# Expert weights in loads of 2 MB, and the conditional part of a mixture-of-experts layer behind pair 10

## The chip, the core and the metric

The kernel runs on one core of one Trainium2 chip. The metric is device time in microseconds for one execution of the whole layer; the median of three runs is given. Engines are TensorE (PE for matmuls, PEld for its weight loads), VectorE (DVE), ScalarE (ACT), GpSimd (POOL) and SyncE (SP); SP issues nearly all transfers from memory.

## What is computed

One layer of a hybrid decoder on 256 tokens of width 1024. A mixer (stick-breaking attention beside an mLSTM, gated and projected) comes first, then a mixture of 32 experts, top 4 of them for each token, then a final RMSNorm. The expert part carries most of the bytes:

```python
def clamped_swiglu_expert(xb, w1, b1, w2, b2):
    a = xb @ w1 + b1
    x_glu, x_lin = jnp.split(a, 2, axis=-1)
    x_glu = jnp.minimum(x_glu, SWIGLU_LIMIT)
    x_lin = jnp.clip(x_lin, -SWIGLU_LIMIT, SWIGLU_LIMIT)
    return ((x_lin + 1.0) * (x_glu * jax.nn.sigmoid(SWIGLU_ALPHA * x_glu))) @ w2 + b2
...
top_logit, top_idx = lax.top_k(logits, TOP_K)
top_w = jax.nn.softmax(top_logit, axis=-1)
...
y = jnp.zeros((n_tok, d), h.dtype).at[row_tok].add((rows * row_w[:, None]).astype(h.dtype))
```

Each expert has `w1` of 1024 x 2048 and `w2` of 1024 x 1024 in float32, 12.6 MB together; all 32 experts are read, 403 MB.

## The kernel before

**Mixer.** Up to about 375 us the kernel computes the mixer. Its weights come through the function `load` into weight buffers of 8 KB per partition (1 MB, called a slot here): 16 in the first stage, then 41 chunks of projection weights and 16 blocks of modulation weights, 73 in all. `next_slot` hands out slots in a fixed rotation over four pools (`ring` 8, `ring2` 4, `ring3` 5, `ring4` 1, and one named `mglo` from `mgp`), 19 at the end. A load into a slot waits until the last reader of what stood there is done. SP issues loads in a fixed order, so one that waits holds up all that stand behind it.

**Experts.** Experts are taken two at a time, 16 pairs. A pair has 24 weight tiles of 1 MB: 8 of `w1` for half 0 of the hidden width (hf 0), 8 for half 1 (hf 1), 8 of `w2` (kt 0 to 7 each). `pair(p)` puts the biases into PSUM (`biases`), runs `first_product` for hf 0 with the scatter of the pair before (`scatter`, behind kt 1 to 4), then hf 1, then gathers the tokens of the next pair (`gather`), then runs `second_product`. One tile feeds four matmuls of 128x512, each recorded as two. Each of the two experts has room for 64 tokens.

**Prefetch for pair 0.** While the router is computed, 16 of the loads of pair 0 are in flight or landed; the two tiles of kt 7 of `w1` go as 256 KB pieces into small buffers of the pool `spl`, and kt 5 of `w2` goes as two pieces into `spare` and `more_rows`.

**Conditional part.** Experts with more than 64 tokens would be served by `more` in two nested loops under `tc.If(rounds > 0)`. Here `rounds` is 0 and nothing of it runs, but each engine loads the number `nit` and branches over the body. Five slots (`ws`) are taken for it. It stands behind pair 14. Ahead of it the scatter of pair 14 runs alone and the eight hf 0 loads of pair 15 are issued. Instructions are reordered by the compiler within the code ahead of the conditional and within the code behind it, not across it.

**Last pair.** Pair 15 is written out by hand: hf 0, the map for its scatter, hf 1, and then `steps`, in which the second product comes in three column groups (512, 256, 256) with the output work of each group (`out_of`) between them, from `w2_last` in pieces of 1 MB and 512 KB. The RMSNorm and the store end the kernel.

Of the kernel before, what the change touches and what calls it, by code (L numbers as in the profile page):

```python
# [13 lines left out]
F32 = mybir.dt.float32  # L14
# [10 lines left out]
D = 1024  # L25
# [38 lines left out]
def body(tc, a, out):  # L64
# [17 lines left out]

    const, c_const = pool("const")
    ring, c_ring = pool("ring", bufs=RING)
    slots, SLOT_NAME = [ring] * RING, {}

    def next_slot(shape):

        p = slots.pop(0)
        slots.append(p)  # L90
        return p.tile(shape, F32, name=SLOT_NAME.get(p, "w"))

    def load(src, shape):
        w = next_slot(shape)
# [585 lines left out]
    moe, c_moe = pool("moe", reuse_waits="tile")  # L680
    xgp, c_xgp = pool("xgp", reuse_waits="tile")
    ring3, c_ring3 = pool("ring3", bufs=RING3, reuse_waits="tile")
    ring4, c_ring4 = pool("ring4", side="right", reuse_waits="tile")
    slots[4:4] = [ring3] * RING3 + [ring4]
    wk, c_wk = pool("wk", reuse_waits="tile")
    table("natural_log_exp_and_others")
    A2 = moe.tile([128, 8], F32, name="A2")
# [201 lines left out]
        act(S, pt[:, 0:T], AF.Copy)  # L889
        SS[p] = S  # L890

    def of_w1(p, hf, kt):

        return load(w1[p, hf, kt], [128, 2, 2, 512])

    def of_w2(p, kt):

        return load(w2[p, kt], [128, 2, D])


    W1 = {(hf, kt): of_w1(0, hf, kt) for kt in range(7) for hf in range(2)}
# [1 line left out]
    for hf in range(2):  # L903
        W1[hf, 7] = [[spl.tile([128, 512], F32, name=("whi", "wlo")[hf]) for b in range(2)] for e in range(2)]
        for e in range(2):
            for b in range(2):
                nc.sync.dma_start(W1[hf, 7][e][b], w1[0, hf, 7, :, e, b])
    for kt in range(2, 5):
        W2[kt] = of_w2(0, kt)
    spare = xgp.tile([128, 1, D], F32, name="xh")  # L910
    nc.sync.dma_start(spare, w2[0, 5, :, 0:1])
    more_rows = next_slot([128, 1, D])
    nc.sync.dma_start(more_rows, w2[0, 5, :, 1:2])

    def biases(p):
        sel = wk.tile([128, 2, CAP], BF16, name="sel", bufs=2)
# [6 lines left out]

    def first_product(p, a1, hf, kt):

        w = W1.pop((hf, kt)) if p in (0, NE // 2 - 1) and (hf, kt) in W1 else of_w1(p, hf, kt)
        for b in range(2):
            for e in range(2):
                pe(a1[2 * b + hf][64 * e:64 * e + 64], XG[p][:, kt, 64 * e:64 * e + 64],
                   w[e][b] if isinstance(w, list) else w[:, e, b], start=False, stop=kt == KT - 1, skip_group_check=True)  # L930

    def second_product(p, a2, aT, kt):
        if p == 0 and kt == 5:
            w = [spare[:, 0], more_rows[:, 0]]
        else:
            w = W2[kt] if p == 0 and kt in W2 else of_w2(p, kt)
# [9 lines left out]
    def pair(p):  # L946
        a1 = biases(p)
        aT = halves([128, 4, 128]) if p else None
        if p == 0:
            for kt in range(KT):  # L950
                gather((kt,), G0, XG[0])
                for hf in range(2):
                    first_product(p, a1, hf, kt)
            scatter_map(p)
            aT = halves([128, 4, 128])
            ms = [hidden(a1, hf) for hf in range(2)]
            G, _ = slots_of(p + 1)
# [27 lines left out]
    def add_b2(b2):  # L985
# [8 lines left out]
    for p in range(NE // 2 - 1):  # L994
        pair(p)
        if p == 1:
            b2 = xgp.tile([128, D], F32, name="xh")[0:32]
            nc.sync.dma_start(b2, a["b2"])
        if p == 3:
            add_b2(b2)  # L1000
# [21 lines left out]
    def more(r, q, e, ws):  # L1022
# [21 lines left out]
        for kt in range(KT):  # L1044
            w = ws[kt % 4]
            for hf in range(2):
                nc.gpsimd.dma_start(w.rearrange("p (b h n) -> p b h n", b=2, h=2)[:, :, hf],
                                    w1[ds(q, 1), hf, kt, :, e].rearrange("q p b n -> p (q b) n"))
            for n in range(4):
                mm(a1[n], xg[kt // 4][:, kt % 4, :], w[:, 512 * n:512 * n + 512], start=False, stop=kt == KT - 1)  # L1050
        aT = activations(a1)
        a2 = [ps1.tile([128, 512], F32, name=f"s{n}") for n in range(2)]
        for kt in range(KT):
            w = ws[kt % 4]
            nc.gpsimd.dma_start(w[:, 0:D], w2[ds(q, 1), kt, :, e].rearrange("q p n -> p (q n)"))
# [5 lines left out]
    ws = [next_slot([128, 2 * D]) for _ in range(5)]  # L1061
    with tc.If(rounds > 0):
        with tc.For_i(0, rounds, 1) as r:
            with tc.For_i(0, NE // 2, 1) as q:
                for e in range(2):
                    more(r, q, e, ws)
# [12 lines left out]
    m = hidden(a1, 1)  # L1079
# [78 lines left out]
    close(c_ring4, c_mgp, c_ps2, c_ps1, c_wk, c_ring3, c_xgp, c_moe, c_ring2, c_mb, c_spl, c_m, c_ring, c_const)  # L1158


RING, RING2, RING3 = 8, 4, 5

LAST = ((0, 512, 2), (512, 256, 4), (768, 256, 2))


def layout(i):
# [28 lines left out]
    o["w1"] = np.ascontiguousarray(n["expert_w1"][0].reshape(16, 2, KT, 128, 2, 2, 512).transpose(0, 5, 2, 3, 1, 4, 6))  # L1195
    o["b1"] = n["expert_b1"][0]
    o["w2"] = np.ascontiguousarray(n["expert_w2"][0].reshape(16, 2, KT, 128, D).transpose(0, 2, 3, 1, 4))
# [22 lines left out]
```

## Time and profile before

| | us |
|---|---|
| median of 3 runs (1326.29 to 1328.52) | 1328.28 |
| the profiled execution, its own time | 1330.19 |
| its span from first to last instruction | 1328.5 |
| PE busy in the span | 1228.4 (92%) |
| DVE / ACT / POOL busy | 468.0 / 329.9 / 30.0 |
| read from memory | 481.21 MB, 363 GB/s over the span |

The profiled execution lies 1.9 us above the median; 1.7 us of its time lie outside the span. A busy PE is one with a matmul in flight, not one at its peak. The DMA share is the mean busy share of the core's 16 DMA engines. A wait for several semaphores is put down to the one that came last. A slice of the page is a fortieth of the span, 33.2 us.

### The profile page before, as it was taken

What the parts mean: (1) busy time and instruction counts of PE and PEld (TensorE: products, weight loads), DVE (VectorE), ACT (ScalarE), POOL (GpSimd) and SP (SyncE); (2) the same over time, 40 slices, a digit from 0 to 9 for tenths busy, and PEclk for the clock granted to TensorE, in tenths of its full rate; (3) what the DMA queues carried; (4) which work ended last, traced back from release to release, by engine and by line L of the source; (5) the groups of instructions that cost most, each with busy time, mean ns of one, the idle gap of its engine ahead of it and who ended that gap; (6) DMA issues with size and microseconds to landing.
All of it is one profiled execution on the core that took longest, in us unless ns stands there. A gap on an engine that the chain in (4) does not pass through costs nothing. (4 is left out here: it accounts for less than half of the span.)

```text
span 1328.5 us, 16889 instructions
## 1 busy us (share of the span) xinstructions
PE 1228.4 (92%) x6859; PEld 668.3 (50%) x6874; DVE 468.0 (35%) x923; ACT 329.9 (25%) x616; POOL 30.0 (2%) x63
## 2 busy tenths in 40 slices
PE   5979999999999999999999999988989898898787
PEld 3878999999963333433334433332333333332323
DVE  5979888776532112122121220212121120201203
ACT  4457767655522010110101101010110101010102
POOL 2000000000000000000000000000000000000002
PEclk8989999999999999999999999999999999999989
DMA  9586476486878999999999999999999999999993
GB/s 342 205 301 254 159 275 235 172 343 245 330 278 361 407 418 420 420 420 420 420 421 420 420 422 419 420 420 420 421 420 421 420 421 420 420 420 420 419 419 151
DMA packets 70337, 483.46 MB, mean 364 GB/s; under 512 B 8134, under 2 KB 9558, under 8 KB 13676
## 3 DMA queue, kind: packets, MB, share of 16 engines
q1 hardware_dynamic: 69084, 480.54, 89.3%
q0 software_dynamic: 624, 1.23, 0.3%
q8 instruction: 57, 0.93, 0.3%
q10 hardware_dynamic: 544, 0.52, 0.1%
q14 instruction: 28, 0.23, 0.0%
HBM read 481.21 MB, written 1.05 MB: 363 GB/s over the span
## 5 line engine op out<-in xcount | busy, mean ns | idle before, releaser
L808 PE MATMUL s<-w,xg 128*64 128x512 f32 x1928 | 450.2, 602 | 31.3 <-DMA w<-in_w 28.1
L808 PEld LDWEIGHTS s<-w,xg 128*64 128x64 f32 x1928 | 125.2, 137 | 296.9 <-issue 207.2
L808 PE MATMUL t<-w,whi 128*64 128x512 f32 x908 | 204.2, 596 | 13.4 <-ACT whi L859 9.6
L825 DVE SCALAR_TENSOR_TENSOR xT<-pm,modT,xT 128x256 f32<-128x256 f32 x128 | 56.0, 479 | 391.1 <-PE pm L808 391.1
L808 PEld LDWEIGHTS t<-w,whi 128*64 128x64 f32 x908 | 61.7, 137 | 133.9 <-issue 103.7
L843 ACT ACTIVATE wlo<-wlo 128x512 f32<-128x512 f32 x32 | 20.2, 630 | 425.3 <-DVE wlo L841 425.3
L222 DVE TENSOR_TENSOR wlo<-w,whi 128x512 fp32r<-128x512 f32 x164 | 110.0, 686 | 44.3 <-ACT whi L220 43.6
L220 ACT ACTIVATE whi<-w 128x512 fp32r<-128x512 f32 x162 | 100.8, 629 | 80.7 <-PE pj L257 61.9
L841 DVE TENSOR_SCALAR wlo<-s 128x512 f32<-128x512 f32 x32 | 22.1, 691 | 249.0 <-PE s L808 227.5
L258 PE MATMUL pj<-hhi,wlo 128*128 128x256 f32 x368 | 104.9, 285 | 0.9 <-DVE wlo L222 0.8
L256 PE MATMUL pj<-hhi,whi 128*128 128x256 f32 x368 | 105.0, 285 | 0.2 <-DVE kp L486 0.2
L257 PE MATMUL pj<-hlo,whi 128*128 128x256 f32 x368 | 104.5, 284 | 0.0
L258 PEld LDWEIGHTS pj<-hhi,wlo 128*128 128x128 f32 x368 | 70.4, 191 | 1.6 <-DVE wlo L222 1.4
L256 PEld LDWEIGHTS pj<-hhi,whi 128*128 128x128 f32 x368 | 70.4, 191 | 0.8 <-DVE kp L486 0.4
L257 PEld LDWEIGHTS pj<-hlo,whi 128*128 128x128 f32 x368 | 70.5, 192 | 0.3 <-issue 0.2
L808 PEld LDWEIGHTS pm<-G,mghi 128*128 128x128 f32 x512 | 59.0, 192 | 17.6 <-issue 17.0
L808 PE MATMUL pm<-S,whi 128*128 128x256 f32 x240 | 67.3, 404 | 0.2 <-DVE xT L825 0.2
L808 PEld LDWEIGHTS pm<-S,whi 128*128 128x128 f32 x240 | 40.8, 189 | 50.0 <-issue 37.1
L808 PE MATMUL pm<-G,mghi 128*128 128x128 f32 x512 | 63.3, 279 | 0.2 <-ACT xg L836 0.2
L169 DVE CUSTOM_DVE_ANT_0 w<-w,silr,col 128x1024 f32<-128x1024 f32 x48 | 60.4, 1278 | 1.1 <-DMA w<-in_ada 0.9
L859 ACT ACTIVATE whi<-pm 128x512 f32<-128x512 f32 x32 | 19.1, 598 | 166.8 <-PE pm L811 166.8
L836 ACT ACTIVATE xg<-pm,modT 128x128 f32<-128x128 f32 x128 | 37.1, 368 | 63.5 <-PE pm L808 63.5
(371 smaller groups left out, 1335.1 us busy)
## 6 DMA issues: line engine op xcount, KB each, us to landing
w<-in_w SPq DMA_DIRECT2D x354, 1024.0 KB, 19.9
w<-in_w_in SPq DMA_DIRECT2D x29, 1024.0 KB, 6.5
w<-in_ada SPq DMA_DIRECT2D x22, 1024.0 KB, 5.6
mglo<-in_w SPq DMA_DIRECT2D x19, 1024.0 KB, 19.9
w<-in_w_first SPq DMA_DIRECT2D x7, 896.0 KB, 12.9
w<-in_w_last SPq DMA_DIRECT2D x5, 1024.0 KB, 19.6
w<-in_w_a SPq DMA_DIRECT2D x4, 1024.0 KB, 5.3
w<-in_w_b SPq DMA_DIRECT2D x4, 1024.0 KB, 12.5
```

Source lines behind the costliest of these rows:

```text
L169: nc.vector.tensor_tensor_reduce(out=w[:, j + n, :], in0=w[:, j + n, :], in1=SILU[-1], scale=1.0, scalar=col[:, C_AB + i:C_AB + i + 1], op ...
L220: act(hi, x, AF.Copy)
L222: nc.vector.tensor_tensor(lo, x, f32(hi), OP.subtract)
L256: mm(ps[:, n, :], whi[:, j, s], mhi[:, kt, :], start=kt + n == 0, stop=False, skip_group_check=True)
L257: mm(ps[:, n, :], whi[:, j, s], mlo[:, kt, :], start=False, stop=False, skip_group_check=True)
L258: mm(ps[:, n, :], wlo[:, j, s], mhi[:, kt, :], start=False, stop=last, skip_group_check=True)
L808: return tc.keep_in_program_order(mm(*args, **kw))
L825: stt(xT[:, kt, :], p[:, j, :], mod_of(G2, kt), xT[:, kt, :], OP.mult, OP.add)
L836: act(xg[kt] if isinstance(xg, list) else xg[:, kt, :], p[:, width * j:width * j + width], AF.Identity, bias=mod_of(SH2, kt))
L841: ts(g, glu, LIMIT, None, op0=OP.min)
L843: act(s, g, AF.Sigmoid, scale=ALPHA)
L859: act(aT[hf], pt.rearrange("p (k m) -> p k m", k=4), AF.Copy)
```

## The change

Weight buffers become 16 KB per partition: `ring` 4, `ring2` 2, `ring3` 3, nine in all; `ring4` is gone, and `mglo` serves once, for kt 4 of `w2` of pair 0. `next_slot` now hands out halves of such a buffer (a wide buffer here), two calls for one; `next_wide` hands out a whole one and drops a half that is left over. `w1` and `w2` are laid out in memory so that two kt stand side by side, 16 KB in a row for each partition. For pairs 1 to 15 `first_product` loads two kt of `w1` in one transfer of 2 MB, and for pairs 1 to 14 `second_product` does so with `w2`. The mixer's loads, those of pair 0 and those of `w2_last` stay at 1 MB or less, into halves.

The conditional part stands behind pair 10. The scatter of pair 10 runs alone ahead of it, and pair 11 has none in its first product. The hand-written prefetch of eight loads for pair 15 is gone; the scatter of pair 14 runs inside hf 0 of pair 15, as in the other pairs, and the map for the scatter of pair 15 moves from behind hf 0 to behind kt 1 of hf 1.

```diff
-    slots, SLOT_NAME = [ring] * RING, {}
+    slots, spare_half = [ring] * RING, []
...
+    def next_wide():
+        spare_half.clear()
         p = slots.pop(0)
         slots.append(p)
-        return p.tile(shape, F32, name=SLOT_NAME.get(p, "w"))
+        return p.tile([128, 4 * D], F32, name="w")
+
+    def next_slot(shape):
+        if not spare_half:
+            w = next_wide()
+            spare_half.append(w[:, 2 * D:])
+            return shaped(w, shape)
+        return shaped(spare_half.pop(), shape)
...
-    slots[4:4] = [ring2] * RING2
+    slots[2:2] = [ring2] * RING2
...
-    ring4, c_ring4 = pool("ring4", side="right", reuse_waits="tile")
-    slots[4:4] = [ring3] * RING3 + [ring4]
+    slots[2:2] = [ring3] * RING3
...
-    SLOT_NAME[mgp] = "mglo"
-    slots.append(mgp)
...
+    def wide_w1(p, hf, k2):
+        w = next_wide()
+        nc.sync.dma_start(w, w1[p, hf, k2].rearrange("p j e b n -> p (j e b n)"))
+        return [shaped(w[:, 2 * D * j:], [128, 2, 2, 512]) for j in range(2)]
+
+    def wide_w2(p, k2):
+        w = next_wide()
+        nc.sync.dma_start(w, w2[p, k2].rearrange("p j e n -> p (j e n)"))
+        return [shaped(w[:, 2 * D * j:], [128, 2, D]) for j in range(2)]
...
-    for kt in range(2, 5):
+    for kt in range(2, 4):
         W2[kt] = of_w2(0, kt)
+    W2[4] = of_w2(0, 4, mgp.tile([128, 2, D], F32, name="mglo"))
...
-        w = W1.pop((hf, kt)) if p in (0, NE // 2 - 1) and (hf, kt) in W1 else of_w1(p, hf, kt)
+        if (hf, kt) not in W1:
+            W1[hf, kt], W1[hf, kt + 1] = wide_w1(p, hf, kt // 2)
+        w = W1.pop((hf, kt))
...
-                if 1 <= kt <= 4:
+                if p - 1 in ROWS and 1 <= kt <= 4:
                     scatter(p - 1, (kt - 1,))
...
-    p = NE // 2 - 1
-    scatter(p - 1)
-    for kt in range(KT):
-        W1[0, kt] = of_w1(p, 0, kt)
...
+    for p in range(NE // 2 - 1):
+        pair(p)
...
+        if p == REST_AT:
+            scatter(p)
+            del ROWS[p]
+            rest_of_slots()
+
+    p = NE // 2 - 1
     a1 = biases(p)
     aT = halves([128, 4, 128])
     for kt in range(KT):
         first_product(p, a1, 0, kt)
-    scatter_map(p)
+        if 1 <= kt <= 4:
+            scatter(p - 1, (kt - 1,))
     m = hidden(a1, 0)
     for kt in range(KT):
         first_product(p, a1, 1, kt)
+        if kt == 1:
+            scatter_map(p)
...
-RING, RING2, RING3 = 8, 4, 5
+RING, RING2, RING3 = 4, 2, 3
+REST_AT = 10
```

`rest_of_slots` holds what stood under the conditional before: five calls of `next_slot` for `ws`, the test and the two loops.

## Rows read from the trace of the kernel before

**Rows 1.** Page, part 2: busy tenths of 40 equal slices of the span
```profile
PE   5979999999999999999999999988989898898787
DMA  9586476486878999999999999999999999999993
GB/s 342 205 301 254 159 275 235 172 343 245 330 278 361 407 418 420 420 420 420 420 421 420 420 422 419 420 420 420 421 420 421 420 421 420 420 420 420 419 419 151
```

**Rows 2.** Windows: stretch, us, busy of each engine, PEclk, DMA share, GB/s
```profile
600.00:1200.00 600.00, 561.34 (x2605) 209.23 (x2614) 110.48 (x233) 64.32 (x152) 2.94 (x10) 1.00 1.01 420
```

**Rows 3.** Waits of the whole run: us in total, times, longest us
```profile
PEld s L808 <- DMA w<-in_w: 83.8, 85, 1.6
...
SPq L95 <- DMA w<-in_w: 600.4, 288, 3.5
```

**Rows 4.** Timeline of PE: start us, us, instructions, idle before them
```profile
442.28 0.81 PE L808 MATMUL s<-b1s,sel 128*128 128x512 bf16 x3 [0.16 <-issue]
...
496.12 0.81 PE L808 MATMUL s<-b1s,sel 128*128 128x512 bf16 x3 [0.16 <-issue]
...
1228.43 1.94 PE L808 MATMUL s<-w,xg 128*64 128x512 f32 x8 [0.55 <-DMA w<-in_w]
```

**Rows 5.** Chain that ended last, in order of time: start us, us, what
```profile
1265.56 17.66 PE s L808 x68
```

**Rows 6.** Timeline around the conditional part, 1248 to 1268 us
```profile
1248.40 17.80 SPq L95 DMA_DIRECT2D w<-in_w  x8
...
1250.25 1.99 PE L808 MATMUL pm<-S,whi 128*128 128x256 f32 x8
...
1259.96 0.98 DVE L884 TENSOR_SCALAR rw<-cst,rank,gate 128x64 f32<-128x64 f32 x4 [4.65 <-PEq L1062]
1265.56 1.87 PE L808 MATMUL s<-b1s,sel 128*128 128x512 bf16 x4 [11.15 <-issue]
```

**Rows 7.** Windows: one stretch of 10 us behind the branch
```profile
1260.00:1270.00 10.00, 4.44 (x12) 1.31 (x14) 0.95 (x4) 0.00 (x0) 0.00 (x0) 0.50 1.02 420
```

**Rows 8.** Windows: the last microseconds of the loads
```profile
1306.00:1308.00 2.00, 2.00 (x20) 1.12 (x16) 0.00 (x0) 0.60 (x1) 0.00 (x0) 1.00 0.33 133
1308.00:1309.00 1.00, 1.00 (x8) 0.69 (x5) 0.00 (x0) 0.00 (x0) 0.00 (x0) 1.00 0.06 25
```

**Rows 9.** Timeline of PE in the last pair's second product
```profile
1302.92 5.38 PE L1105 MATMUL t<-w,whi 128*64 128x512 f32 x32 [0.69 <-ACT whi L859]
...
1310.15 3.67 PE L1105 MATMUL t<-w,whi 128*64 128x256 f32 x32
...
1314.82 1.95 PE L1105 MATMUL t<-w,whi 128*64 128x256 f32 x16
```

**Rows 10.** DMA queues, 600 to 1200 us: packets, MB, share; loads: KB, us to landing
```profile
q1 hardware_dynamic: 34557, 251.66, 101.0%
q8 instruction: 21, 0.34, 0.2%
...
w<-in_w SPq DMA_DIRECT2D x226, 1024.0 KB, 19.9
```

**Rows 11.** DMA queues, 1323 to 1328 us, where the output is stored
```profile
q10 hardware_dynamic: 544, 0.52, 32.0%
q1 hardware_dynamic: 544, 0.52, 31.5%
```

**Rows 12.** Timeline of SP, 414 to 430 us
```profile
414.53 14.45 SPq L95 DMA_DIRECT2D w<-in_w  x3
```

**Rows 13.** Windows: one microsecond in pair 0
```profile
427.00:428.00 1.00, 1.00 (x6) 0.29 (x4) 0.27 (x2) 0.92 (x4) 0.00 (x0) 1.00 0.00 0
```

**Rows 14.** The tile nit: duration ns min/median/max, first and last start us
```profile
L1015 DVE CAST nit<-cnt x1: 143/143/143, 386.2 to 386.2; 1x1 int32<-1x1 f32 x1
...
L1016 SPq TENSOR_LOAD <-nit x1: 486/486/486, 1248.8 to 1248.8; - x1
...
L1016 PEldq TENSOR_LOAD <-nit x1: 494/494/494, 1253.2 to 1253.2; - x1
```

More of the change, by code (lines that the diff above doesn't have):

```diff
@@ L84, in body, with shaped @@
     ring, c_ring = pool("ring", bufs=RING)
-    slots, SLOT_NAME = [ring] * RING, {}
-    def next_slot(shape):
+    slots, spare_half = [ring] * RING, []
+    def shaped(x, shape):
+        n = int(np.prod(shape[1:]))
+        names = "abc"[:len(shape) - 1]
+        x = x[:, 0:n]
+        if len(names) == 1:
+            return x
+        return x.rearrange(f"p ({' '.join(names)}) -> p {' '.join(names)}", **dict(zip(names[1:], shape[2:])))
+    def next_wide():
+        spare_half.clear()
         p = slots.pop(0)
         slots.append(p)
-        return p.tile(shape, F32, name=SLOT_NAME.get(p, "w"))
+        return p.tile([128, 4 * D], F32, name="w")
[5 more added lines that the diff above has]
+        return shaped(spare_half.pop(), shape)
     def load(src, shape):
@@ L890, in scatter_map, with of_w1, of_w2 @@
         SS[p] = S
[L892 to L898, printed above, removed]
+    def of_w1(p, hf, kt, w=None):
+        w = next_slot([128, 2, 2, 512]) if w is None else w
+        nc.sync.dma_start(w, w1[p, hf, kt // 2, :, kt % 2])
+        return w
+    def of_w2(p, kt, w=None):
+        w = next_slot([128, 2, D]) if w is None else w
+        nc.sync.dma_start(w, w2[p, kt // 2, :, kt % 2])
+        return w
+    def wide_w1(p, hf, k2):
[6 more added lines that the diff above has]
+        return [shaped(w[:, 2 * D * j:], [128, 2, D]) for j in range(2)]
     W1 = {(hf, kt): of_w1(0, hf, kt) for kt in range(7) for hf in range(2)}
@@ L906, in body @@
             for b in range(2):
-                nc.sync.dma_start(W1[hf, 7][e][b], w1[0, hf, 7, :, e, b])
-    for kt in range(2, 5):
+                nc.sync.dma_start(W1[hf, 7][e][b], w1[0, hf, 3, :, 1, e, b])
+    for kt in range(2, 4):
         W2[kt] = of_w2(0, kt)
+    W2[4] = of_w2(0, 4, mgp.tile([128, 2, D], F32, name="mglo"))
     spare = xgp.tile([128, 1, D], F32, name="xh")
-    nc.sync.dma_start(spare, w2[0, 5, :, 0:1])
+    nc.sync.dma_start(spare, w2[0, 2, :, 1, 0:1])
     more_rows = next_slot([128, 1, D])
-    nc.sync.dma_start(more_rows, w2[0, 5, :, 1:2])
+    nc.sync.dma_start(more_rows, w2[0, 2, :, 1, 1:2])
     def biases(p):
@@ L935, in second_product @@
         else:
-            w = W2[kt] if p == 0 and kt in W2 else of_w2(p, kt)
+            if kt not in W2:
+                if p:
+                    W2[kt], W2[kt + 1] = wide_w2(p, kt // 2)
+                else:
+                    W2[kt] = of_w2(p, kt)
+            w = W2.pop(kt)
             w = [w[:, e] for e in range(2)]
@@ L992, in add_b2 @@
         add_out(lambda kt: b2[:, 128 * kt:128 * kt + 128], gT)
[L994 to L1000, printed above, removed]
-    p = NE // 2 - 1
-    scatter(p - 1)
-    for kt in range(KT):
-        W1[0, kt] = of_w1(p, 0, kt)
     rest = moe.tile([128, 2, 2, NE], F32, name="rest")
@@ L1047, in more @@
                 nc.gpsimd.dma_start(w.rearrange("p (b h n) -> p b h n", b=2, h=2)[:, :, hf],
-                                    w1[ds(q, 1), hf, kt, :, e].rearrange("q p b n -> p (q b) n"))
+                                    w1[ds(q, 1), hf, kt // 2, :, kt % 2, e].rearrange("q p b n -> p (q b) n"))
             for n in range(4):
@@ L1054, in more @@
             w = ws[kt % 4]
-            nc.gpsimd.dma_start(w[:, 0:D], w2[ds(q, 1), kt, :, e].rearrange("q p n -> p (q n)"))
+            nc.gpsimd.dma_start(w[:, 0:D], w2[ds(q, 1), kt // 2, :, kt % 2, e].rearrange("q p n -> p (q n)"))
             for n in range(2):
@@ L1059, in more, with rest_of_slots @@
         add_out(lambda kt: block(rows, kt), S)
[L1061 to L1066, printed above, removed]
+    def rest_of_slots():
+        ws = [next_slot([128, 2 * D]) for _ in range(5)]
+        with tc.If(rounds > 0):
+            with tc.For_i(0, rounds, 1) as r:
+                with tc.For_i(0, NE // 2, 1) as q:
+                    for e in range(2):
+                        more(r, q, e, ws)
+    for p in range(NE // 2 - 1):
+        pair(p)
+        if p == 1:
+            b2 = xgp.tile([128, D], F32, name="xh")[0:32]
+            nc.sync.dma_start(b2, a["b2"])
+        if p == 3:
+            add_b2(b2)
+        if p == REST_AT:
[3 more added lines that the diff above has]
+    p = NE // 2 - 1
     a1 = biases(p)
@@ L1157, in body @@
         eng.dma_start(out[256 * g:256 * g + 256, :].rearrange("(j p) t -> p j t", p=128), xo[:, 2 * g:2 * g + 2, :])
-    close(c_ring4, c_mgp, c_ps2, c_ps1, c_wk, c_ring3, c_xgp, c_moe, c_ring2, c_mb, c_spl, c_m, c_ring, c_const)
-RING, RING2, RING3 = 8, 4, 5
+    close(c_mgp, c_ps2, c_ps1, c_wk, c_ring3, c_xgp, c_moe, c_ring2, c_mb, c_spl, c_m, c_ring, c_const)
+RING, RING2, RING3 = 4, 2, 3
+REST_AT = 10
 LAST = ((0, 512, 2), (512, 256, 4), (768, 256, 2))
@@ L1193, in layout @@
     o["router_w"] = np.ascontiguousarray(n["router_w"][0].reshape(KT, 128, NE).transpose(1, 0, 2))
-    o["w1"] = np.ascontiguousarray(n["expert_w1"][0].reshape(16, 2, KT, 128, 2, 2, 512).transpose(0, 5, 2, 3, 1, 4, 6))
+    o["w1"] = np.ascontiguousarray(n["expert_w1"][0]
+                                   .reshape(16, 2, KT // 2, 2, 128, 2, 2, 512).transpose(0, 6, 2, 4, 3, 1, 5, 7))
     o["b1"] = n["expert_b1"][0]
-    o["w2"] = np.ascontiguousarray(n["expert_w2"][0].reshape(16, 2, KT, 128, D).transpose(0, 2, 3, 1, 4))
+    o["w2"] = np.ascontiguousarray(n["expert_w2"][0]
+                                   .reshape(16, 2, KT // 2, 2, 128, D).transpose(0, 2, 4, 3, 1, 5))
     last = n["expert_w2"][0][NE - 2:].reshape(2, KT, 128, D)
```

## Prediction

> **What bounds the kernel now.** Start with the 40 slices of the page [rows 1]. Up to slice 12 (about 400 us) PE is full and the transfers are not; from slice 15 on the transfers run at 420 GB/s, a DMA share of 1.01 [rows 2], nearly to the end. So there are two stages with different limits: the mixer goes by its engines, the experts by bytes. The waits confirm it [rows 3]: PE's weight loads wait 83.8 us in all for expert weights, and SP's longest wait, 600 us, is for earlier transfers to land. A pair is 24 tiles of 1.049 MB; at 420 GB/s that is 59.9 us. What PE needs for a pair is read where it does not wait: the biases of pair 1 begin at 442.28 and those of pair 2 at 496.12, so 53.8 us [rows 4]. PE therefore starts pair 1 with loads in hand, uses them up at 6.1 us a pair, and waits from about pair 8 on: 0.55 us ahead of a tile's matmuls at 1228, where these matmuls take 1.94 [rows 4].
>
> The end is different. The chain that ended last is PE alone from 1265.56 us [rows 5], although transfers went on to about 1309 (share 0.06 in the microsecond before it) [rows 8]. The reason is the conditional part [rows 6]: the scatter of pair 14 begins at 1250.25, PE is over the branch just before 1259.96 (a VectorE instruction waits for that), and its next matmul comes at 1265.56 after 11.15 us without one. Then it runs at a granted clock of 0.50, the 1.2 GHz level, in most of 1260 to 1270 [rows 7]. SP is not held: its eight loads from 1248.40 on have the usual distance [rows 6], and the share stays 1.02 [rows 7]. So the branch costs only because it stands too near the end for PE to make it up.
>
> **The conditional moved.** Moving it behind pair 10 moves five register loads and branches, one on each engine, the lone scatter, and five buffers; its own transfers, on POOL's queue, are in the body and do not run. The price on PE is the same there: from the scatter's start to the first bias 15.3 us [rows 6], of which the scatter (two runs of 2 us) is work that pair 11 then lacks, so some 12 us, and about 3 more for the half clock: 15. Queued behind PE's branch are the biases of pair 11; DVE and ACT wait for PE. What makes it up is PE's slack: 59.0 us a pair after the change (below) less 53.8, so 5.2 a pair. Three pairs repay 15 us; four (11 to 14) stand before pair 15. Transfers must not stop meanwhile. When the last load of pair 10 lands (call it 0), six wide buffers outside `ws` can hold pair 11: 12.6 MB, 29 us. The three under `ws` can be loaded once PE has passed the branch: 3.4 us for the last two tiles and 9.7 from the scatter's start to 1259.96 [rows 6], so 13. The cover is 16 us. SP reaches its branch some eight loads ahead of PE, and the number it tests has been ready since 386 us [rows 14]; it read it 4.4 us before PE did. Cost: 0, and 14 if that cover fails (below). The few DVE steps that make the number stay ahead of pair 0: under 1 us, taken as 0. The prefetch of eight loads is removed with nothing late: pair 15's loads stand in line anyway.
>
> At the end PE now follows the loads. Let E be the last landing, 1309. Behind the first 1 MB piece of the second column group come 3 MB more, 7.5 us at 420 GB/s, so it lands at E - 7.5. From there PE has 1.84 (half of 3.67) + 1.85 (gap between the first two rows) + 1.84 + 1.84 + 1.0 (next gap) + 1.95 [rows 9] = 10.3 us: the second product ends at E + 2.8, 1311.8, against 1316.8 now. The output behind it is unchanged. Gain 4.9; I take **-4.7**, since the shared landing of kt 6 and 7 makes hf 1 end a little later. Bounds: 0 if PE has not caught up, -6.9 if only the last two matmul groups (0.9 us) stood behind E. The scatter of pair 14 goes into hf 0 and the map behind kt 1, as in every pair; both lie beside waits for loads.
>
> **2 MB in one load.** From 600 to 1200 us queue 1 took 34557 packets and 251.66 MB in 101.0% of 16 engines' 600 us, 9696 us [rows 10]. Nearly all data packets are one 8 KB row; 16 small ones per load tell of its landing. The store of the output at the end has 1 KB rows: 544 packets, 0.524 MB, 25.4 us (mean of two queues, 32.0% and 31.5% of 16 x 5 us) [rows 11]. Two equations, packets x a + MB x b, give a = 11 ns a packet and b = 37.0 us a MB. The share is 1.0% over full, 2.8 ns a packet, so packets overlap by that much and 8.2 ns count. A 2 MB load with 16 KB rows has 144 packets instead of 288, 9 fewer on each engine: 74 ns. Pairs 1 to 14 have 12 such loads and pair 15 eight, 176; five are issued before the transfers become the limit. 171 x 74 ns = **-12.6 us**, 0.9 a pair. Upper end: a = 11 in full, 99 ns, -16.9. Lower end: if a 16 KB row still goes as two packets, only the landing notes are saved, 1 packet an engine, -1.4. Below that: the trace's only 16 KB packets are 21 instruction fetches at 0.2% of 9600 us, 0.9 us each [rows 10], against 0.56 for two rows of 8 KB. They end elsewhere and run between the loads' own packets, so I do not scale by them, but a loss is not excluded (rival 3). I take 74 ns because the store's rows and the loads' rows are both plain copies on these queues.
>
> The Trainium skill, "DMA: Bandwidth & Descriptors", section "Why small descriptors are slow (HBM only)", speaks of a fixed cost of about 3 cycles a packet and finds saving it worth while only for small descriptors. At the 850 MHz that the page gives for the fabric this is an estimate of 3.5 ns, 32 ns a load, 5.4 us in place of 12.6, and the sum would be 1320.7, inside rival 1; the 11 ns from these rows speak against so low a price.
>
> In flight there are eight loads: 19.9 us to landing [rows 10] over 2.5 us for one. With nine wide buffers about eight remain, twice the bytes.
>
> **Wide buffers ahead of the limit.** A wide buffer is free only when both halves are. In the mixer a first half waits for one chunk more; behind that load stands all of SP's queue. What hides it is that PE is full there and the transfers idle in part [rows 1], so I take 0; if a chunk comes late, PE stands for one 2 MB transfer, 5.0 us, each time (rival 2). In pair 0 the transfers run dry: share 0.00 at 427 to 428 [rows 13], since SP's three issues from 414.53 stretch over 14.45 us [rows 12], waiting for the first `w2` tiles to be used. At such a point only the number of freed tiles counts. Before the experts 73 halves are handed out, an odd number, so the first tile of pair 0 shares with the last chunk, and its last `w1` tile shares with the first of `w2`: one tile less is free. The loads lose one tile's time, 1.049 MB at 420 GB/s: **+2.5 us**. That kt 3 of `w2` must wait for the first tile's use ends in the same dry spell, so it adds nothing. Bounds 0 and 5.
>
> **Sum.** 1328.5 - 4.7 - 12.6 + 2.5 = 1313.7 span; with 1.7 outside it 1315.4 for an execution like the profiled one, which is 1.9 above the median: **1313.5**.
>
> **Rivals.**
> 1. *Long rows are hardly cheaper.* If a row still goes as two packets the gain is 1.4 instead of 12.6: 1324.7; if more of a packet's 8.2 ns overlaps in a full stream than the 101.0% shows, so that a third to a half counts, it is 4 to 6: 1320 to 1322. For it: packets overlap already, and the trace has no such row on this queue. Against: the two equations. 18%.
> 2. *The mixer slips.* One or two chunks come 5 us late: 1319 to 1324. For it: DVE and ACT go in a fixed order and every half waits for its partner. Against: PE stays full while the share is 0.5 to 0.9. 16%.
> 3. *Long rows slow the stream*, the case on the other side. Without a gain the sum is 1326.1; it becomes slower than now by 0.2% once a 2 MB load costs 28 ns (0.6%) more than two of 1 MB. At 1% more, 50 ns x 171 = 8.6: 1334.7. For it: the 0.9 us above. Against: nothing shows a row's cost to grow faster than its bytes. 10%.
> 4. *SP is held at the conditional until PE has passed.* Nothing of pair 11 would be in flight at 0, and the transfers stand for 13 us and a start of about 1: 1327.5. Against: SP passed at once before [rows 6, 14]. 8%.
>
> **Chances.** The forecast has 48%, 1307 to 1319 by its own bounds (-4.3 for the full 11 ns, -2.2 for the tail, +4.7 if PE is late). The range 1307 to 1328 also holds rivals 1, 2 and 4 and leaves out rival 3 and the extremes. Within 0.2% (2.7 us) a measurement of this kernel can hardly tell a change from none. Below 1325.6 are the forecast, rival 2 and most of rival 1: 76% faster, 12% the same, 12% slower.
>
> **What would show it.** Right: queue 1 with half the packets between 600 and 1200 us and more than 420 GB/s (426); 2 MB loads landing some 39 us after their issue; PE's gap of 11 to 12 us near 1005 us with the share still 1.01; PE waiting for loads in pair 15; loads ending near 1299 and the second product 3 us later. Wrong: a packet count unchanged (rival 1), a rate below 420 (rival 3), a share under 1 behind pair 10 (rival 4), PE idle before 375 us (rival 2).

## The result and the profile after

The kernel after takes **1320.84 us** (median of 5 runs, 1319.34 to 1321.56) against 1328.30 us for the kernel before beside it (1326.29 to 1330.71): a ratio of **0.9938, 95% interval 0.9926 to 0.9949**, 0.6% faster. The forecast was 1313.5 us with a range of 1307 to 1328. The sign and the range hold; the time came out 7.3 us above the number, and above the 1319 that the forecast's own bounds reach: the range holds it only because it was made wide for three rivals. The profiled execution took 1320.84 us with a span of 1319.2 us, where the sum had a span of 1313.7: 5.5 us of the 7.3 lie in the span, and 1.9 come from the step from the profiled execution to the median, for here the profiled one is the median.

| | before | forecast | after |
|---|---|---|---|
| span of the profiled execution, us | 1328.5 | 1313.7 | 1319.2 |
| queue 1 in 600 to 1200 us, packets | 34557 | half | 17562 |
| transfers there, GB/s | 420 | 426 | 427 |
| last weight load landed, us | 1309.1 | 1299 | 1304.1 |
| from there to the end of the span, us | 19.4 | 14.7 | 15.1 |

The page of the kernel after, part 2, answers to [rows 1]: busy tenths of PE and of the transfers in 40 equal slices, and what these moved.

```profile
PE   4989999999989999999999999989887999989887
...
DMA  9675556496669899999999999999999999999995
GB/s 337 216 269 223 225 209 258 173 382 241 256 225 418 354 416 428 427 426 426 428 428 426 429 427 427 427 426 427 428 426 425 426 427 427 427 428 428 427 423 212
```

The same two stages: from slice 16 up to the last but one the transfers run at 423 to 429 GB/s where it was 419 to 422, and the last slice holds more of them (212 for 151), since the loads now end nearer the end. The queues between 600 and 1200 us, for [rows 10]: packets, MB and share of 16 engines' time; below, the loads with their KB and the us to landing.

```profile
q1 hardware_dynamic: 17562, 255.70, 100.3%
...
w<-in_w SPq DMA_DIRECT2D x124, 2048.0 KB, 37.5
```

Half the packets, 1.6% more bytes in the same time. The chain that ended last, for [rows 5], in order of time (start us, us, what):

```profile
1021.76 20.48 PE s L823 x84
...
1057.57 7.02 PE t L823 x32
1069.55 37.10 DMA w<-in_w
...
1269.88 27.09 DMA w<-in_w_last
```

Before, PE alone was the chain from 1265.56 us on. Now PE holds it only from the conditional part behind pair 10 to 1069.5 us; then the transfers hold it to their end. The timeline of PE at the end, for [rows 9] (start us, us, instructions, idle before):

```profile
1284.59 3.65 PE L823 MATMUL s<-w,xg 128*64 128x512 f32 x16 [1.26 <-DMA w<-in_w]
...
1305.47 1.95 PE L1146 MATMUL t<-w,whi 128*64 128x256 f32 x16
```

and the windows of the last loads, for [rows 8]:

```profile
1302.00:1304.00 2.00, 2.00 (x22) 1.35 (x20) 0.69 (x1) 0.63 (x2) 2.00 (x3) 1.00 0.28 113
1304.00:1305.00 1.00, 1.00 (x9) 0.56 (x6) 0.00 (x0) 0.00 (x0) 0.66 (x1) 1.00 0.00 0
```

PE waits for weights in pair 15, the loads end at 1304.1 us (share 0.00 behind it), and the second product ends 3.4 us later, at 1307.4; the forecast had 2.8 behind the last landing. So the end does what was forecast, 5 us late. Where were these 5 us lost? The start of pair 0 tells. First PE in the kernel before, whose rows were not shown above:

```profile
381.89 0.38 PE L151 MATMUL t<-onesb 128*128 128x512 bf16 x1
382.11 1.02 PE L808 MATMUL s<-b1s,sel 128*128 128x512 bf16 x3
...
384.03 3.65 PE L808 MATMUL s<-w,xg 128*64 128x512 f32 x16 [0.46 <-ACT xg L836]
```

and the same place of the kernel after:

```profile
382.54 0.38 PE L169 MATMUL t<-onesb 128*128 128x512 bf16 x1
386.92 1.01 PE L823 MATMUL s<-b1s,sel 128*128 128x512 bf16 x2 [4.00 <-DVE rw L899]
...
390.10 4.22 PE L823 MATMUL s<-w,xg 128*64 128x512 f32 x16 [0.46 <-ACT xg L851]
```

The mixer's last product starts 0.65 us later (382.54 for 381.89). Then PE stands for 4.00 us where it had not stood at all, and its first expert products take 4.22 us in place of 3.65. The row puts the wait down to VectorE's `rw`, but the bias product reads nothing of `rw`. What PE has in its queue there is seen under the tile `nit` (engine, operation, duration in ns, first and last start in us), to be set against [rows 14]:

```profile
L1039 DVE CAST nit<-cnt x1: 133/133/133, 386.2 to 386.2; 1x1 int32<-1x1 f32 x1
L1040 PEldq TENSOR_LOAD <-nit x1: 483/483/483, 386.4 to 386.4; - x1
L1040 SPq TENSOR_LOAD <-nit x1: 478/478/478, 394.6 to 394.6; - x1
L1040 POOLq TENSOR_LOAD <-nit x1: 482/482/482, 953.7 to 953.7; - x1
L1040 ACTq TENSOR_LOAD <-nit x1: 467/467/467, 1011.5 to 1011.5; - x1
L1040 DVEq TENSOR_LOAD <-nit x1: 543/543/543, 1015.6 to 1015.6; - x1
```

The change leaves `rounds = nc.values_load(nit, ...)` where `nit` is made, and moves the loop over the pairs behind both; so the read of `nit` into PE's register stands in PE's queue ahead of the first bias. `nit` is written at 386.2 us, PE reads it at 386.4 and goes on at 386.9. Before, the read stood behind pair 14, at 1253.2 us [rows 14], when the number was 867 us old. The reads of POOL, ACT and DVE come from the same line of code, but run between 953 and 1016 us, towards the branch: of the five, only PE's and SP's run early in the kernel after.

### The profile page after: what moved, and what is told of

Same layout as the page of the kernel before. It is cut to its first block, busy times and chain, and to the rows that moved or that the text cites. A ratio compares the mean times of both kernels' runs of the same rounds, so it can differ in the third digit from the quotient of the medians.

```text
span 1319.2 us, 16510 instructions
## 1 busy us (share of the span) xinstructions
PE 1224.6 (93%) x6859; PEld 675.7 (51%) x6874; DVE 467.9 (35%) x923; ACT 330.8 (25%) x616; POOL 32.3 (2%) x63
## 5 line engine op out<-in xcount | busy, mean ns | idle before, releaser
L823 PE MATMUL s<-w,xg 128*64 128x512 f32 x2032 | 465.2, 601 | 30.3 <-DMA w<-in_w 27.0
L823 PEld LDWEIGHTS s<-w,xg 128*64 128x64 f32 x2032 | 135.6, 137 | 298.8 <-issue 244.7
L823 PE MATMUL t<-w,whi 128*64 128x512 f32 x948 | 212.3, 596 | 11.7 <-ACT whi L874 9.6
L823 PEld LDWEIGHTS t<-w,whi 128*64 128x64 f32 x948 | 65.1, 137 | 137.1 <-issue 114.0
```

The costliest lines, as they stand in the source:

```text
L823: return tc.keep_in_program_order(mm(*args, **kw))
```

## Experiments

Theory A: the 5.5 us are the price of this read on PE, and the four other steps of the sum hold. Theory B: the read is harmless, and the wide buffers' missing tile costs more than the 2.5 us forecast. Every time is a median, with its ratio to the kernel before run beside it; us in the text are ratio times 1329.

| run | time, us | ratio to before, 95% |
|---|---|---|
| kernel after | 1320.84 | 0.9938 (0.9926 to 0.9949) |
| after, late read | 1314.06 | 0.9876 (0.9859 to 0.9892) |
| before, early read | 1335.72 | 1.0047 (1.0034 to 1.0059) |
| before, conditional behind pair 10 | 1325.12 | 0.9966 (0.9954 to 0.9978) |
| late read, conditional behind pair 14 | 1322.20 | 0.9943 (0.9931 to 0.9956) |
| late read, and PE alone reads early too | 1320.32 | 0.9935 (0.9920 to 0.9950) |
| late read, and an early read in the code for the four others | 1314.12 | 0.9887 (0.9871 to 0.9903) |
| PE alone reads early, products in the wait | 1317.68 | 0.9915 (0.9900 to 0.9931) |
| late read, conditional behind pair 13 | 1317.28 | 0.9906 (0.9890 to 0.9922) |
| late read, three loads in another order | 1314.72 | 0.9889 (0.9874 to 0.9905) |
| late read, two loads of 1 MB a buffer | 1327.15 | 0.9975 (0.9962 to 0.9987) |
| late read, 2 MB loads, rows of 8 KB | 1327.97 | 0.9977 (0.9964 to 0.9989) |
| late read, 2 MB loads, rows of 4 KB | 1351.30 | 1.0160 (1.0143 to 1.0177) |

**The late read.** The kernel after, with one line moved:

```diff
-    rounds = nc.values_load(nit, min_val=0, max_val=2)      # ahead of pair 0
...
     def rest_of_slots():
         ws = [next_slot([128, 2 * D]) for _ in range(5)]
+        rounds = nc.values_load(nit, min_val=0, max_val=2)
```

> The kernel after, but the five engines read nit (the number of further rounds) into a register just ahead of the conditional, behind pair 10, and not ahead of pair 0; nit is still computed ahead of pair 0. Theory A (the 5.5 us that the result came out above the forecast's span are the wait of 4.00 us in which TensorE, at the start of pair 0, stands before its read of nit; it delays the release of the first weight buffer and the stream idles 6.57 us there, where the forecast had 2.5): the stream's idle time at 387 us falls to about 2.5 us, 1315 to 1316.5 us. Theory B (the missing tile alone makes the dry spell, and the wait is repaid behind it): 1319.5 to 1321 us.

It took 1314.06 us, 16.5 us under the kernel before and 8.2 under the kernel after, a little below the 1315 to 1316.5 expected: theory A, and a version that beats both kernels. Its span is 1313.6 us; the profiled execution is the slowest of its four, 1.2 us above the median. PE at the start of pair 0:

```profile
383.21 0.38 PE L169 MATMUL t<-onesb 128*128 128x512 bf16 x1
383.43 1.02 PE L823 MATMUL s<-b1s,sel 128*128 128x512 bf16 x3
...
385.35 3.65 PE L823 MATMUL s<-w,xg 128*64 128x512 f32 x16 [0.46 <-ACT xg L851]
```

No wait, and 3.65 us as before. The windows there (stretch, us, busy of PE, PEld, DVE, ACT, POOL, then PEclk, DMA share, GB/s), first of the kernel after:

```profile
384.00:388.00 4.00, 1.01 (x2) 0.40 (x3) 2.82 (x14) 0.00 (x0) 0.00 (x0) 0.56 0.50 210
388.00:392.00 4.00, 3.39 (x11) 1.76 (x12) 0.00 (x0) 0.37 (x1) 0.29 (x1) 0.59 0.02 4
```

and the same windows of the run with the late read:

```profile
384.00:388.00 4.00, 3.49 (x20) 1.53 (x20) 3.56 (x16) 0.37 (x1) 0.29 (x1) 1.00 0.77 309
388.00:392.00 4.00, 3.54 (x20) 1.40 (x18) 0.00 (x0) 0.37 (x1) 0.00 (x0) 1.00 0.93 287
```

Two things are read here. With PE's idle time the granted clock is 0.56 and 0.59, that is at the 1.2 GHz level for most of these 8 us; without it it stays 1.00. And the transfers stop (share 0.02), because SP's next load waits for the first weight buffer that PE frees; with the late read they hardly stop here at all (0.77 and 0.93), where the expectation had left 2.5 us of idle time.

How a wait of 4 us on PE reaches an end that the transfers set is seen at the second stop of the stream, near 430 us, where all buffers are full and SP waits for PE to use pair 0's second weights. SP's waits from 415 to 432 us in the kernel before (us in total, times, longest):

```profile
SPq L95 <- PE t L808: 13.3, 2, 12.0
```

The windows about the end of that stop, first of the kernel before:

```profile
427.50:429.50 2.00, 2.00 (x12) 0.72 (x10) 0.00 (x0) 0.42 (x2) 0.00 (x0) 1.00 0.00 0
429.50:430.00 0.50, 0.50 (x4) 0.14 (x2) 0.00 (x0) 0.00 (x0) 0.00 (x0) 1.00 0.98 131
```

of the kernel after:

```profile
433.50:436.00 2.50, 2.50 (x14) 0.79 (x12) 0.41 (x2) 1.05 (x4) 0.00 (x0) 1.00 0.00 0
436.00:437.00 1.00, 1.00 (x8) 0.36 (x6) 0.00 (x0) 0.00 (x0) 0.00 (x0) 1.00 1.11 213
```

and of the run with the late read:

```profile
428.50:430.50 2.00, 2.00 (x12) 0.69 (x10) 0.09 (x1) 0.74 (x3) 0.00 (x0) 1.00 0.00 0
430.90:432.00 1.10, 1.10 (x8) 0.38 (x6) 0.00 (x0) 0.00 (x0) 0.00 (x0) 1.00 1.27 238
```

By the transfers' own records the stream starts again at 429.61, 436.24 and 430.95 us. Against the start of the mixer's last product (381.89, 382.54, 383.21) that is 47.7, 53.7 and 47.7 us. In all ten kernels without an early read on PE this distance is 47.7 to 47.8; the early read adds 6.0 here. Until that point PE sets the pace of the buffers, so what PE loses before it is lost to the stream, in full.

**The early read in the kernel before.** The block that makes `nit`, and its read, put ahead of the loop over pairs; nothing else:

```diff
     nc.vector.tensor_copy(nit, cnt[0:1, 1:2])
     rounds = nc.values_load(nit, min_val=0, max_val=2)
+    for p in range(NE // 2 - 1):
+        pair(p)
...
```

> The kernel before with one thing of the change: nit is computed and read into the engines' registers ahead of pair 0; the conditional stays behind pair 14 and the loads stay 1 MB. Theory A (TensorE waits about 4 us for its read of nit, and pair 0 starts that much later): pair 0's first bias product at 386 us instead of 382.1 us; with the four loads that stand in the queue at that time as cover, the stream loses 0 to 3 us, so 1328 to 1331.5 us. Theory B (the read costs nothing wherever it stands): 1328 us and the first bias product at 382.1 us.

PE in that run:

```profile
387.09 1.01 PE L808 MATMUL s<-b1s,sel 128*128 128x512 bf16 x2 [4.01 <-DVE rw L884]
```

The wait is the same, 4.01 us. The time rose by 6.2 us (4.5 to 7.8), more than the 0 to 3 expected: I had counted the four loads in SP's queue as cover. They do cover the first stop, but not the one near 430 us: from the mixer's last product to the stream's second start it is 54.4 us, 6.7 more than before.

**Which engine's read.** In the version with the late read, one more read of `nit` ahead of pair 0, once on PE alone (shown here), once on the four other engines:

```diff
+    nc.values_load(nit, (mybir.EngineType.PE,), min_val=0, max_val=2)
     for p in range(NE // 2 - 1):
         pair(p)
```

> The kernel with the late read, with one more read of nit ahead of pair 0 on TensorE alone. Theory A (TensorE's own read is what delays pair 0): a wait of about 4 us ahead of the first bias product, the clock at half behind it, 1320 to 1322 us as in the kernel after. Rival (the read on one of the other engines, SyncE's ahead of the load queue above all): 1314 us.

> The kernel with the late read, with one more read of nit ahead of pair 0 on the four engines other than TensorE. Theory A: 1313.5 to 1315 us, the first bias product 0.2 us behind the router's last product. Rival (SyncE's read, which stands ahead of later loads): 1319 to 1322 us.

PE alone gives 1320.32 us, the kernel after's time, the four others 1314.12 us, the late read's. The row of the first, PE:

```profile
386.23 1.88 PE L823 MATMUL s<-b1s,sel 128*128 128x512 bf16 x4 [4.43 <-DVE rw L899]
```

So 6.4 us (0.9935 against 0.9887) hang on PE's read. In the second run only SP's early read is in the trace, at 388.1 us; DVE, ACT and POOL show one read each, from 946 us on, as in the kernel after. So that run tries SP alone: its early read costs nothing. What an early read on the three others would cost was not tried, and the kernel after has none.

**The wait and the clock.** The run with PE's early read, with products on unused data ahead of it:

```diff
+    for _ in range(18):
+        pe(idle, onesb, onesb[:, None, :].to_broadcast([128, 4, 128]), start=True, stop=True)
     nc.values_load(nit, (mybir.EngineType.PE,), min_val=0, max_val=2)
```

> The run with the early read on TensorE alone (1320.3 us), with 18 products of 512 columns on unused data put on TensorE ahead of that read, about as long as the wait. In that run the stall took 4.4 us and pair 0 was 1.9 us longer than without the read, at a granted clock of 0.50 in its first us. Theory A (the 6.2 us are a wait of 4.4 us and 1.9 us of half clock behind it): the wait stays, as products in place of idle time, the clock stays at 1.00, pair 0 has its 60 us again, and the time falls by 1.5 to 2.5 us to 1318 to 1319 us. Rival (the clock costs nothing at the end, the place of the buffers' release alone counts): 1320 to 1321 us.

PE at the start of pair 0 in that run:

```profile
380.76 4.05 PE L823 MATMUL t<-onesb 128*128 128x512 bf16 x18
385.32 1.03 PE L823 MATMUL s<-b1s,sel 128*128 128x512 bf16 x3 [0.52 <-issue]
...
387.25 3.65 PE L823 MATMUL s<-w,xg 128*64 128x512 f32 x16 [0.46 <-ACT xg L851]
```

The first bias comes as late as ever (4.8 us behind the mixer's last product, 380.54), but the clock stays 1.00, the first products take 3.65 us, the stream's second start comes 52.3 us after the mixer in place of 54.2, and the time falls by 2.7 us (0.9915 against 0.9935; expected were 1.5 to 2.5). The two intervals overlap, so the times alone do not show a gain; the 1.9 us in the traces do. So of the 6.4 us some 4.5 are the wait and 2 the half clock.

**The conditional part alone.** The kernel before with the conditional and the read behind pair 10, the scatter of pair 14 inside pair 15, loads as before:

```diff
+        if p == REST_AT:
+            scatter(p)
+            del ROWS[p]
+            rest_of_slots()
...
-    scatter(p - 1)
-    for kt in range(KT):
-        W1[0, kt] = of_w1(p, 0, kt)
```

> The kernel before with one thing of the change: the conditional stands behind pair 10, with nit read there, and the second scattering of pair 14 inside pair 15; the loads stay 1 MB with rows of 8 KB. Theory A (the 15 us that TensorE loses at the conditional are repaid over the following three pairs, so that only the part beyond the last load leaves the end): 4.7 us less, 1323.6 us. Rival (SyncE is held at the conditional long enough to idle the stream): 1327 us or more.

4.5 us less (2.9 to 6.1): the forecast's term of 4.7 holds, and SP was not held (share 1.01 and 411 GB/s between 1010 and 1016 us, while PE stood). The traces say the same more sharply than the times: from the end of the loads to the end of the span it is 15.1 to 15.2 us here and in every other run with the conditional behind pair 10, with rows of 4, 8 or 16 KB, against 19.4 in the kernel before.

**The conditional back behind pair 14**, in the version with the late read, with the first half of pair 15's first weights loaded ahead of it:

```diff
+    scatter(p - 1)
+    del ROWS[p - 1]
+    for kt in range(0, KT, 2):
+        W1[0, kt], W1[0, kt + 1] = wide_w1(p, 0, kt // 2)
+    rest_of_slots()
```

> The kernel after with the conditional put back behind pair 14 (nit read there, the first half of pair 15's first weights loaded ahead of it as before), loads of 2 MB with rows of 16 KB. Theory A (loads and conditional are two separate terms, and the late read takes the pair 0 wait away): against the run with the late read alone, 4 to 6 us more, 1320 to 1321 us. Rival (with the shorter stream, TensorE's lag at the end grows by what the stream gains): the loads' gain is lost at the end, 1326 to 1328 us.

1322.20 us, 8.9 us above the late read: more than the 4 to 6 expected, less than the rival's. The loads end at the same time as with the late read (1298.4 us in both), and from there to the end of the span it is 22.0 us in place of 15.1; so in these two executions the whole difference is PE behind the loads. PE in that run:

```profile
1253.02 0.59 PE L823 MATMUL s<-b1s,sel 128*128 128x512 bf16 x1 [7.49 <-PEq L1087]
1258.56 1.46 PE L823 MATMUL s<-b1s,sel 128*128 128x512 bf16 x3 [4.96 <-issue]
```

From the scatter's start at 1241.37 to the second of these rows it is 17.2 us, 1.9 more than in the kernel before. The loads end 10.7 us earlier than before (1309.1 to 1298.4), PE's second product of the last pair starts only 8.1 us earlier (1302.92 in [rows 9] to 1294.78). The difference fits these 1.9 us and the 0.9 that the loads still win in the pair behind the stall. The two terms of the sum are therefore not independent. Alone the conditional gives 4.5, the loads (with their missing tile) 7.6, together 16.5: behind faster loads a stall near the end costs more.

**The conditional behind pair 13** (`REST_AT = 13`, late read):

> The kernel with the late read, with the conditional behind pair 13 in place of pair 10. The forecast's account: TensorE loses about 15 us there and has 2 pairs with some 5 us of idle time each to win it back, so that about 5 us are left at the last load, and behind pair 14 about 10: the run with the conditional behind pair 14 was 8 us over this one, so some 3 us more here, 1316 to 1319 us. Rival (the whole lag shows wherever it stands less than three pairs from the end): 1322 us.

1317.28 us, 2.5 us above the run measured beside it, in which SP reads early: as expected, though the two intervals overlap. The traces are clearer: from the end of the loads to the end of the span it is 17.5 us, against 15.1 behind pair 10 and 22.0 behind pair 14, and behind the branch PE never waits for a load for more than 0.3 us. So two pairs are too few for the stall there. But PE stands longer at that place (11.55 us, against 6.17 behind pair 10 in the kernel after), so this does not show how many pairs the stall behind pair 10 needs.

**The order of three loads.** In pair 0, the load for the first buffer to be freed issued behind the two whose buffers are free earlier:

```diff
-    for kt in range(2, 4):
-        W2[kt] = of_w2(0, kt)
+    W2[2] = of_w2(0, 2)
     W2[4] = of_w2(0, 4, mgp.tile([128, 2, D], F32, name="mglo"))
     spare = xgp.tile([128, 1, D], F32, name="xh")
     nc.sync.dma_start(spare, w2[0, 2, :, 1, 0:1])
+    W2[3] = of_w2(0, 3)
```

> The kernel with the late read, with the load that waits for the first free buffer (the fourth of pair 0's second weights) issued behind the two loads beside it whose buffers are free earlier. Theory A (the missing tile costs 2.7 us of stream in pair 0, read from the bytes left at 395 us): 2 to 3 us less, 1311 to 1312.5 us. Rival (the bytes are lost again at the next dip of the stream near 428 us): 1314 us.

Two windows of that run:

```profile
388.00:392.00 4.00, 3.54 (x18) 1.41 (x20) 0.00 (x0) 0.37 (x1) 0.00 (x0) 1.00 1.02 419
424.00:428.00 4.00, 3.72 (x26) 2.76 (x28) 2.88 (x8) 2.35 (x9) 0.00 (x0) 1.00 0.00 0
```

No gain (0.9889 against 0.9887): the stream is full at 388 to 392, where the late read had 287 GB/s, and stops earlier, at 424 in place of 428 us. The rival holds. What counts is what the buffers hold when the stream stops: queue 1's packets, MB and share from that stop to the end, of the kernel before (from 428.5 us):

```profile
q1 hardware_dynamic: 51136, 366.63, 98.4%
```

of the kernel after (from 435 us):

```profile
q1 hardware_dynamic: 26656, 367.67, 98.2%
```

and of the late read (from 429.5 us):

```profile
q1 hardware_dynamic: 26656, 367.67, 98.3%
```

1.04 MB more are left to load: one tile, 2.5 us at 420 GB/s. The order of the loads cannot change that.

**What the long rows are worth.** Three runs on the version with the late read: each buffer of 16 KB filled by two loads of 1 MB; one load of 2 MB with the weights in memory such that a partition's part is two pieces of 8 KB; the same with four of 4 KB.

```diff
-        nc.sync.dma_start(w, w1[p, hf, k2].rearrange("p j e b n -> p (j e b n)"))
+        for j in range(2):
+            nc.sync.dma_start(w[:, 2 * D * j:2 * D * j + 2 * D], w1[p, hf, k2, :, j].rearrange("p e b n -> p (e b n)"))
...
```

```diff
-                                   .reshape(16, 2, KT // 2, 2, 128, 2, 2, 512).transpose(0, 6, 2, 4, 3, 1, 5, 7))
+                                   .reshape(16, 2, KT // 2, 2, 128, 2, 2, 512).transpose(0, 6, 2, 3, 4, 1, 5, 7))
...
-        nc.sync.dma_start(w, w1[p, hf, k2].rearrange("p j e b n -> p (j e b n)"))
+        nc.sync.dma_start(w.rearrange("p (j x) -> p j x", j=2), w1[p, hf, k2].rearrange("p j e b n -> p j (e b n)"))
...
```

> The kernel with the late read (loads of 2 MB with rows of 16 KB, 1314 us), with each 2 MB buffer of the pair loop filled by two loads of 1 MB with rows of 8 KB. Theory A (what the loads gain hangs on the number of packets, that is on the length of the rows, and 16 KB rows saved 12.6 us by the forecast and 14 us by the trace): 1326 to 1328 us. Theory B (the gain came from the new arrangement of buffers and has nothing to do with the transfers): 1313 to 1316 us.

> The kernel with the late read, loads of 2 MB as there, but the weights lie in memory so that each partition's part of a load is two pieces of 8 KB. Theory A (rows): 1326 to 1328 us, as with two loads of 1 MB. Theory C (the size of a transfer, fewer and larger ones): 1313 to 1316 us. In between: both have a share.

> As the run with 8 KB pieces, with the weights in memory as four pieces of 4 KB for each partition of a 2 MB load. Theory A with a fixed price for a packet: from 16 to 8 KB a packet is added for each 16 KB, from 8 to 4 KB two more, so three times the 12.6 to 14 us: 1352 to 1356 us. Theory D (below 8 KB a packet's price is hidden): under 1335 us.

1327.15, 1327.97 and 1351.30 us. Two loads of 1 MB and one of 2 MB with the same rows cost the same (0.9975, 0.9977), so the size of the transfer is worth nothing that these runs can tell (their intervals are 1.7 us to either side), and the length of the rows is the whole gain: 11 to 13 us against the runs with rows of 16 KB (0.9876 to 0.9889). From 8 to 4 KB it is 24.3 us more (0.9977 to 1.0160), about twice as much for twice as many packets added; the expectation had twice 12.6 to 14, and 1351.30 lies just under its 1352. Queue 1 over the whole run, from the page of the late read:

```profile
q1 hardware_dynamic: 43740, 480.53, 88.3%
```

of the run with rows of 8 KB in loads of 2 MB:

```profile
q1 hardware_dynamic: 66268, 480.53, 88.9%
```

and of the run with rows of 4 KB:

```profile
q1 hardware_dynamic: 114012, 480.53, 90.2%
```

The same bytes. From 8 to 4 KB there are 47744 packets more. 2688 of them belong to 21 tiles of pair 0, whose rows are halved too and which are loaded ahead of the stream's second start, where PE still sets the pace; the other 45056 are 2816 on each of 16 engines: 24.3 us / 2816 = 8.6 ns a packet. From 16 to 8 KB, 22528 packets, 1408 on each, and 11.7 to 13.4 us (0.9889 and 0.9876 to 0.9977): 8.3 to 9.5 ns.

## Why the prediction was right, and what it missed

- **The bound** was read rightly: bytes from pair 1 on, PE at the end. The chain of the kernel after goes over to the transfers and ends 15.1 us behind them (14.7 in the sum).
- **The conditional, -4.7 us:** 4.5 measured alone. Its cost of 0 behind pair 10 holds, but by other numbers than in its working. "The price on PE is the same there" was wrong: the stall is 10.3 us, from the scatter's start at 1011.42 to the bias at 1021.76, not 15.3, and PE's gap 6.2 us, not 11 to 12. PE waits for a load again at 1096.88 us, in pair 12, so it has made the stall up in little more than a pair, where three had been counted. It is in the run behind pair 13 that the repayment is seen to matter.
- **The loads, -12.6 us:** right, and by the mechanism named. The price a packet, worked out from the one place of the trace with short rows, was 8.2 ns; the runs give 8.3 to 9.5. In the profiled executions the way from the stream's second start to the last landing went from 879.5 us (429.61 to 1309.1) to 867.8 (436.24 to 1304.06): 11.7 less, which is 14.2 saved if 2.5 are given back for the tile: 1.6 more than the term. The times of the runs with rows of 8 KB put it at 11 to 13, so the term is right within what was measured.
- **The missing tile, +2.5 us:** right, in bytes (1.04 MB) and in its reason; its time was not measured by itself. That the load which must wait for the first tile's use adds nothing was right too, as the run with another order shows.
- **What failed is the sentence "The few DVE steps that make the number stay ahead of pair 0: under 1 us, taken as 0".** It priced the steps that write `nit` and not those that read it. The working let the five register reads move behind pair 10 with the branches; in the diff the read stays where the number is made, ahead of pair 0. There it makes PE wait 4.0 us for VectorE, with all of pair 0's products behind the read in its queue, and the clock falls. Some 6 us were to be added: 6.0 in the two traces, 6.2 to 8.2 in the times. With the read late the median is 1314.06 us, against the 1313.5 of the sum; that the spans agree to 0.1 us (1313.7 and 1313.6) is in part chance, for the start of pair 0 alone lies 1.3 us later in that trace than in the kernel before.
- **That the range held is luck in part.** The forecast's own bounds end at 1319. The range reached 1328 for rivals 1, 2 and 4, none of which came about, and it covered by that a term nobody had thought of.
- **The account of the span:** second start of the stream +6.6 us (0.65 from the mixer, 6.0 from the read), the way to the last landing -11.7, from there to the end -4.3 (19.4 to 15.1); together -9.3 before rounding, 1328.5 to 1319.2.
- **The rivals.** The time lies where rivals 1 and 2 had theirs (1320 to 1324.7 and 1319 to 1324), and neither is the reason. Rival 1 falls by half the packets at 427 GB/s, rival 2 by PE's last mixer product, 0.65 us late where the traces of all runs spread over 4.3 us (378.97 to 383.29), rivals 3 and 4 by the rate and by the share of 1.00 to 1.01 from 1010 to 1070 us. A time that fits a rival says little until its own row has been looked up.
- The Trainium skill, "DMA: Bandwidth & Descriptors", section "Why small descriptors are slow (HBM only)", gives about 3 cycles a packet, from which the estimate was 3.5 ns and a sum of 1320.7 us, almost the measured time. The runs with rows of 16, 8 and 4 KB decide against that price, with 8.3 to 9.5 ns; the agreement was chance.

## What to carry to other kernels

When code is moved, list each engine that reads what it makes, and look in the trace at when the number is written and when each engine reads it: here the one line of code ran early on two of five engines, and on PE, which was the busiest, it waited like any other operand. Such a read belongs just ahead of the branch. A stream-bound kernel may still be paced by an engine until its buffers have first turned over; here what was lost before that point was lost in full, and a few spare buffers did not hide it. Where a transfer's rate is the bound, count packets, not transfers: here the length of the contiguous row was the whole gain, and the size of the load nothing.

## What the runs showed of the hardware

- **A packet's price is much the same from 4 to 16 KB**, 8.3 to 9.5 ns on each engine at a share of 1.01 to 1.02. The stream runs at 427, 420 and 409 GB/s with rows of 16, 8 and 4 KB, by the windows from 600 to 1200 us, of the late read:

```profile
600.00:1200.00 600.00, 562.69 (x2636) 217.00 (x2644) 112.21 (x237) 64.30 (x152) 2.93 (x10) 0.99 1.01 427
```

of the run with rows of 8 KB:

```profile
600.00:1200.00 600.00, 556.14 (x2596) 213.12 (x2594) 108.93 (x229) 64.40 (x152) 2.96 (x10) 0.99 1.01 420
```

and of the run with rows of 4 KB:

```profile
600.00:1200.00 600.00, 535.00 (x2502) 204.97 (x2500) 108.44 (x227) 61.46 (x145) 2.96 (x10) 0.99 1.02 409
```

- **The same branch has two prices on PE.** Behind pair 10 PE goes on 0.2 us after VectorE, which the branch releases (kernel after):

```profile
1021.59 0.98 DVE L899 TENSOR_SCALAR rw<-cst,rank,gate 128x64 f32<-128x64 f32 x4 [5.09 <-PEq L1087]
...
1021.76 1.87 PE L823 MATMUL s<-b1s,sel 128*128 128x512 bf16 x4 [6.17 <-PEq L1087]
```

  Behind pair 13 or 14 it stands 5.6 to 5.9 us more (1259.96 to 1265.56 in [rows 6]; 1193.61 to 1199.48 with the conditional behind pair 13), or stops a second time for 4.96 us behind its first product, as shown above. Queue 8, which fetches instructions, moves blocks of 16 KB at each of these places. In the kernel before two of them start 5.8 us apart (1257.3 and 1263.1 us), and PE goes on 1.4 us after the end of the second; with the conditional behind pair 13 it is the same (1191.0 and 1197.0, PE at 1199.48). With the late read, behind pair 10, two also start 5.7 us apart (1013.9 and 1019.6), but PE goes on at 1016.73, 1.7 us after the end of the first. That fits a branch that lands where a second block is needed at once in the one case and not in the other; where it lands was not looked at, and the cause stays open.
- The Trainium skill, "Runtime: NRT & Kernel Launch", section "Instruction fetch mechanics", calls the cost of crossing a block of 16 KiB mostly hidden, but warns that a taken branch to a place outside the two blocks at hand has to fetch first. This case's traces agree as far as they go: PE stood 5.7 to 12.5 us at the branch in the fourteen traces, with fetches of queue 8 beside it.
